# A one-layer decoder trunk on one core: compressed weights turned in a scores' bank, query splits in other slots, the first MLP chunk's groups in turn, the last factors taken in later, and products of zeros first

## The chip, the cores and the metric

The kernel runs on one core of a Trainium2 chip, as one program. The metric is device microseconds of one execution, as a median over runs. Engines are TensorE (PE; its weight loads are listed as PEld), VectorE (DVE), ScalarE (ACT), GpSimd (POOL) and SyncE (SP), which mostly issues DMAs. All times are in microseconds.

## What is computed

The input x is 512 tokens by 1024 channels, float32, one layer:

```python
h = rms_norm(x, norm_mix[l])
proj = h @ w_in[l]
u, q, kc, vc, ksl, vsl, kwn, vwn, g_nsa, g_merge = jnp.split(proj, IN_SPLITS, axis=-1)
y_pool = pool_mixer(u, w_pool[l], pool_scale[l])
y_nsa = nsa_mixer(q, kc, vc, ksl, vsl, kwn, vwn, g_nsa, ...)
merged = g_a * (y_pool @ w_proj_pool[l]) + g_b * (y_nsa @ w_proj_nsa[l])
x = x + merged @ w_out[l]
h = rms_norm(x, norm_mlp[l])
x = x + jnp.square(jax.nn.relu(h @ w_ff1[l])) @ w_ff2[l]
return rms_norm(x, norm_final)          # after the layer
```

The second mixer has 16 heads of 64 channels in 2 key groups and three branches: compressed keys and values (31 blocks of 32 tokens), selected blocks and a window, each with its softmax and gate. With 8 blocks of 64 tokens and up to 16 to be selected, every causal block is taken, so both other branches are causal attention over all 512 tokens, with keys of their own. The MLP has a hidden width of 4096.

## The kernel before

Every float32 operand of a product is split in two: a high part (fp32r) and a low part, the rest. A product is three matmuls: high by high, high by low, low by high. ACT writes the high part (`wh`, lines 304 and 350) and DVE the low part (`wl`, lines 306 and 352; POOL does some of these while `mode["pool"]` is set). A weight arrives by DMA in a tile `raw`, is split by `emit_prep_half` some steps before its use, and is taken by `use`.

The code is written as generators in a list `side`; `step_side` lets each of them make one step, up to its next `yield`. How many yields stand between two operations sets how far apart they are written. A scheduler then orders the instructions of each engine, and each engine runs its own in that order.

The stages, in order:

1. Start. x arrives, `ones` by `grow` (line 521) spreads the first norm's gain over 128 partitions in PSUM (`psM`), DVE scales x by it, PE turns x (line 548) and the first products follow (line 450).
2. Projections of `w_in`, 128 output channels at a time: 24 matmuls of 128x512 each (line 393). The last of them are left over as filler (`fill`) for the attention stage. A query is rotated (`rope`, with DMAs that swap quarters, `rs<-rx`) and split (`split_q`: ACT line 654, DVE line 656).
3. Attention, 8 pairs of heads with 12 slots each. Slot i: scores on PE in a bank of tag S (`score_pe`, line 1024; S has three banks), the mask and the smallest on DVE (`smax`, line 1049), the exponential on ACT (`expo`), the scale by gate and sum on POOL (`weight`, line 1075). LAG slots later PE turns the weights in a bank of tag T (`turn_pe`, line 1092; T has two banks), ACT and DVE split them (`PT`, lines 1103 and 1107), and PLAG later come the products with the values (`pv`, line 1126). Compressed branch: `cmp_scores` of the next pair starts at slot 4 of each pair; eight small matmuls (line 961), the softmax on DVE, ACT and POOL (lines 968 to 987, into `PC`, high and low part), then four transposes (line 993) and a copy by ACT (`pc`, one buffer), which `pv` takes with `VC` (line 1117) as the first product of a pair's halves. Filler matmuls are spread over the slots by count.
4. The projection of the attention's output, the merge, the output product and the second norm.
5. The MLP in 4 chunks of the hidden width, each with 2 groups. Both MLP products are done over 2 by 2 blocks with seven block products instead of eight, on sums of blocks; products are called A11, A12, S1, S2, S3, S4, A22. In the first product (`Group`, line 1395) sums of the input T1 to T4, in the second (`Wide`, line 1512) sums of the hidden blocks (`yT1` to `yT4`), are made by DVE and split again. For the first chunk the order of block products is in `FIRST`, for the others in `IN_TURN`:

```python
FIRST = ("A11", "A12"), ("S1", "S3", "S2"), ("A22", "S4")
IN_TURN = ("A11", "S3", "S1", "S2", "A12", "A22", "S4")
```

6. The end. `Wide.take` adds finished block products to x (lines 1529 and 1533), `fold` the sums (line 1540), `gained` (POOL, line 1574) multiplies a part of x by the last norm's gain, and per 128 tokens the square sums, the root, the last scale and the store follow.

Of the kernel before, what the change touches and what calls it, by code (L numbers as in the profile page):

```python
# [13 lines left out]
F32 = mybir.dt.float32  # L14
FR = mybir.dt.float32r
# [5 lines left out]
S = 512  # L21
DFF = 4096
NH = 16
NPAIR = NH // 2
# [38 lines left out]
def trunk(ctx: ExitStack, tc: tile.TileContext, A, out):  # L63
# [73 lines left out]
    LAST = 3  # L137
# [53 lines left out]
    for c in range(4):  # L191
        of = [add_group(1, c, g) for g in range(2)]
        if c == 0:
            turn = [(g, o) for os in FIRST[:1] for o in os for g in range(2)]
            turn += [(g, o) for os in FIRST[1:] for g in range(2) for o in os]
        else:
            turn = [(g, o) for g in range(2) for o in IN_TURN]
        add_turn(1, c, of, turn)
        of = [add_group(2, c, g) for g in range(2)]
        seen = {}  # L200
        turn = []
        for o in OUT_TURN if c < LAST else [o for o in LAST_TURN for g in range(2)]:
            g = seen.get(o, 0)
            seen[o] = g + 1
            turn.append((g, o))
        add_turn(2, c, of, turn)
# [310 lines left out]
    identR = cp.tile([128, 128], FR, name="identR")  # L517
    POOL.memset(ones, 1.0)
    psg = [ps1.tile([128, 512], F32, tag="M", bufs=2, name="psM") for _ in range(2)]
    for h in range(2):  # L520
        PE.matmul(psg[h], ones, grow[:, 512 * h:512 * h + 512], start=True, stop=True)

# [123 lines left out]

    Q_BUFS = 4

    def split_q(p, q):

        t = ap.tile([128, 2, S], FR, tag="Q", bufs=Q_BUFS, name="Q")
        for h in range(2):
            r, c = slice(64 * h, 64 * h + 64), slice(64 - 64 * h, 128 - 64 * h)
            ACT.activation(t[r, h, :], q[r, :], AF.Copy)
            yield
            DVE.tensor_tensor(t[c, h, :], q[r, :], t[r, h, :].bitcast(F32), op=ALU.subtract)
            yield
        Q[p] = t

    def turned_q(p):  # L660
# [5 lines left out]
        return None if p < Q_BUFS else oT[:, p, :]  # L666

    def later_q(p):
        yield from split_q(p, oT[:, p, :])

    with ExitStack() as c1:
        p1 = c1.enter_context(pool("p1"))
# [228 lines left out]
    with ExitStack() as c2:  # L901
        p2 = c2.enter_context(pool("p2"))
        ps2 = c2.enter_context(pool("ps2", space=PSUM))
        def fill2():
            for k in FILL2:
                i = int(k[-1])

                def post(ps, i=i, a=k[1] == "a"):
                    if not a:
                        ACT.activation(GB[:, i, :], ps, AF.Tanh, scale=0.5)  # L910
                        return
                    ACT.activation(ps, ps, AF.Tanh, scale=0.5)
                    DVE.scalar_tensor_tensor(MA[:, i, :], ps, 1.0, MA[:, i, :], op0=ALU.add, op1=ALU.mult)
                yield from fm(k, ps2, post)
            free.append(True)
            split_ready()
            early[0] = use("pn0") + (ps2.tile([128, S], F32, tag="F", bufs=F_BANKS, name="psF"),)
            for k in range(7):
                while (k, 1) not in split:
                    yield True  # L920
                proj_k(early[0], k)
                if k % 2 or k == 6:
                    ahead()
                    yield
# [31 lines left out]
        def cmp_scores(p):  # L956
            g = p // 4
            ps = ps2.tile([128, NT, 2, 64], F32, tag="S", bufs=S_BANKS, name="psC")
            for qb in range(NT):
                for h in range(2):  # L960
                    PE.matmul(ps[:, qb, h, :], Q[p][:, h, 128 * qb:128 * qb + 128], KC[g], start=True, stop=True,
                              skip_group_check=True)
            w = p2.tile([128, NT, 2, 64], F32, tag="cw", bufs=1, name="cw")
            s8 = p2.tile([128, 3, 8], F32, tag="c8", bufs=1, name="c8")
            cm = cst[:, C_CM:C_CM + 128].rearrange("p (q n) -> p q n", q=NT)
            wl = w[:, :, :, 0:32]
            wf = w.rearrange("p q h n -> p (q h) n")[:, :, 0:32]
            DVE.tensor_tensor(wl, ps[:, :, :, 0:32], cm[:, :, None, :].to_broadcast([128, NT, 2, 32]), op=ALU.add)
            sc = ps.rearrange("p q h n -> p (q h) n")[:, :, 0:32]
            DVE.tensor_tensor(ps[:, :, :, 0:32], ps[:, :, :, 32:64], wl, op=ALU.add)  # L970
            yield
            DVE.tensor_reduce(s8[:, 0, :], sc, axis=AX.X, op=ALU.min)
            DVE.tensor_tensor(wf, sc, s8[:, 0, :, None].to_broadcast([128, 8, 32]), op=ALU.subtract)
            yield
            yield
            yield
            ACT.activation(wl, wl, AF.Exp, scale=-1.0)
            yield
            DVE.tensor_reduce(s8[:, 1, :], wf, axis=AX.X, op=ALU.add)
            DVE.reciprocal(s8[:, 2, :], s8[:, 1, :])  # L980
            r = s8[:, 2, :].rearrange("p (q h) -> p q h", q=NT)
            DVE.tensor_tensor(r, r, GT[:, :, 6 * p:6 * p + 6:3], op=ALU.mult)
            yield
            POOL.tensor_tensor(wl, wl, r[:, :, :, None].to_broadcast([128, NT, 2, 32]), op=ALU.mult)
            pH, pL = (PC[:, :, e, :].rearrange("p q (h n) -> p q h n", h=2) for e in range(2))
            POOL.tensor_scalar(pH, wl, 1.0, 1.0, op0=ALU.mult, op1=ALU.mult)
            POOL.tensor_tensor(pL, wl, pH.bitcast(F32), op=ALU.subtract)
            for _ in range(6):
                yield
            pt = ps2.tile([128, S], F32, tag="T", bufs=T_BANKS, name="psT")  # L990
            for qb in range(NT):
                src = PC[:, qb, :, :].rearrange("p e c -> p (e c)")
                PE.transpose(pt[:, 128 * qb:128 * qb + 128].bitcast(FR), src, identR)
            t = p2.tile([128, S], FR, tag="pc", bufs=1, name="pc")
            ACT.activation(t, pt, AF.Copy)
            PTc[p] = t
# [152 lines left out]
        for i in range(n + LAG + PLAG):  # L1149
            if i < n:  # L1150
                p = slots[i][0]
                if i % 12 == 11 and Q_BUFS <= p + 2 < NPAIR:
                    side.append(later_q(p + 2))
                assert i % 12 != CMP_AT or p + 1 == NPAIR or p + 1 in Q
                if i % 12 == CMP_AT and p + 1 < NPAIR:
                    side.append(cmp_scores(p + 1))
# [330 lines left out]
    class Wide:  # L1487
# [33 lines left out]

        def take(self, o, ps):
            yield
            for f in range(2):
                if o in ("A11", "S2"):
                    if o == "A11" and self.c == 0:
# [18 lines left out]
    for c in range(4):  # L1545
        Y = Hidden()
        gs = [Group(c, g, Y) for g in range(2)]
        if c == 0:
# [3 lines left out]
            while not turned[0]:  # L1552
                step_side()
            for os in FIRST[1:]:
                for g in gs:
                    for o in os:
                        g.pe(o)
        else:
            for g in gs:
# [20 lines left out]
    def ending():  # L1580
# [4 lines left out]
        DVE.tensor_tensor(x, x, wide.ps["d"][1], op=ALU.add)  # L1585
        for t in (2, 3):
            square_sum(t, 1, 1)
            gained(t, 1)
            yield
        while "A12" not in wide.done:  # L1590
            yield
        for t in (0, 1):
            square_sum(t, 0)
            gained(t, 0)
            yield
        while "A22" not in wide.done:
            yield
        for t in (0, 1):
# [70 lines left out]
```

## Time and profile before

| | |
|---|---|
| median of 3 runs | 796.45 us (795.88 to 797.59) |
| the profiled execution | 794.17 us, with a span of 792.4 us |
| instructions | 12818 |
| PE, PEld, DVE, ACT, POOL busy | 98%, 85%, 78%, 62%, 23% of the span |
| DMA | 142.33 MB, mean 180 GB/s |

The profile is of one execution by the hardware profiler; its row starts count from the span's start. A row of the timeline has the start, the duration, engine, line, operation, output <- input, shapes and count, and in brackets the idle time of the engine just before it with what ended that. Rows of one group that follow each other are joined (x4). Matmuls are pipelined: the duration of one (0.40 for 128x512) is longer than the distance to the next (0.23), and ends are modelled. In what follows a row of a waits list has the total, the count and the longest wait. The costliest groups of PE, DVE, ACT and POOL, with busy time and mean ns of one, then the idle time before them:

```profile
L393 PE MATMUL psF<-R,wh 128*128 128x512 f32 x512 | 165.1, 402 | 0.0
L306 DVE TENSOR_TENSOR wl<-raw,wh 128x1024 fp32r<-128x1024 f32 x75 | 93.0, 1242 | 22.5 <-ACT wh L304 22.4
L304 ACT ACTIVATE wh<-raw 128x1024 fp32r<-128x1024 f32 x75 | 79.2, 1058 | 83.0 <-PE psB L1512 30.3
L1075 POOL TENSOR_SCALAR P<-P,sm,GT 128x128 f32<-128x128 f32 (+3 forms) x128 | 82.7, 674 | 52.7 <-DVE sm L1065 33.3
```

### The profile page before, as it was taken

Reading aid. Unit: us, or ns where it says so; the run is one execution under the profiler, and the core shown is the slowest. Engines: PE = TensorE matmul, PEld = TensorE weight load, DVE = VectorE, ACT = ScalarE, POOL = GpSimd, SP = SyncE. Lnnn points to the kernel's source line nnn. Section 1 sums busy time; section 2 is a strip of 40 time slices with the busy share of each in tenths; the row PEclk is TensorE's granted clock in tenths of the full one; section 3 lists DMA queues with packets and bytes.
Section 4 is the critical chain, followed back from the end, with each engine's and each line's share of the span. In section 5 each row is a group of like instructions: output and inputs, shape, how many; then the busy total and the mean of one; then the engine's idle time right before and its main releaser. Section 6 shows DMA issues by size and latency. Waiting matters only on the chain. (4 is left out here: it accounts for less than half of the span.)

```text
span 792.4 us, 12818 instructions
## 1 busy us (share of the span) xinstructions
PE 775.0 (98%) x4541; PEld 674.0 (85%) x4541; DVE 620.2 (78%) x1176; ACT 489.2 (62%) x962; POOL 181.2 (23%) x246
## 2 busy tenths in 40 slices
PE   8999999999999999999999999999999999999995
PEld 6889877888888888888888899978997899799974
DVE  6888666445999888887655579997889788978897
ACT  6756543335998888896334575944773477347744
POOL 4000000025876665664100100101110110100002
PEclk9999999999999999999999999999999999999998
DMA  9554743487753344334966607999999997987552
GB/s 306 136 153 120 197 110 100 127 213 185 134 108 81 81 95 120 80 81 115 300 155 198 163 1 199 331 238 289 281 262 233 288 282 217 276 240 241 175 171 107
DMA packets 116154, 142.33 MB, mean 180 GB/s; under 512 B 5525, under 2 KB 88121, under 8 KB 115898
## 3 DMA queue, kind: packets, MB, share of 16 engines
q1 hardware_dynamic: 97690, 117.72, 46.1%
q0 software_dynamic: 18112, 23.07, 19.3%
q10 hardware_dynamic: 288, 0.72, 0.3%
q8 instruction: 36, 0.59, 0.3%
q14 instruction: 28, 0.23, 0.1%
HBM read 136.77 MB, written 48.23 MB: 233 GB/s over the span
## 5 line engine op out<-in xcount | busy, mean ns | idle before, releaser
L393 PE MATMUL psF<-R,wh 128*128 128x512 f32 x512 | 165.1, 402 | 0.0
L304 ACT ACTIVATE wh<-raw 128x1024 fp32r<-128x1024 f32 x75 | 79.2, 1058 | 83.0 <-PE psB L1512 30.3
L271 POOL DMA_DIRECT2D S<-w_ff x44 | 48.7, 1107 | 356.5 <-DMA S<-w_ff 240.5
L350 ACT ACTIVATE wh<-raw 128x512 fp32r<-128x512 f32 (+1 forms) x100 | 60.1, 620 | 85.5 <-PE psF L393 45.4
L306 DVE TENSOR_TENSOR wl<-raw,wh 128x1024 fp32r<-128x1024 f32 x75 | 93.0, 1242 | 22.5 <-ACT wh L304 22.4
L393 PEld LDWEIGHTS psF<-R,wh 128*128 128x128 f32 x512 | 92.3, 188 | 17.9
L393 PE MATMUL psF<-R,wl 128*128 128x512 f32 x256 | 101.2, 395 | 0.0
L1075 POOL TENSOR_SCALAR P<-P,sm,GT 128x128 f32<-128x128 f32 (+3 forms) x128 | 82.7, 674 | 52.7 <-DVE sm L1065 33.3
L352 DVE TENSOR_TENSOR wl<-raw,wh 128x512 fp32r<-128x512 f32 (+1 forms) x84 | 56.9, 684 | 26.0 <-ACT wh L350 25.8
L1059 ACT ACTIVATE P<-P,sm 128x128 f32<-128x128 f32 (+3 forms) x128 | 71.0, 557 | 8.1 <-DVE sm L1049 7.5
L1049 DVE CUSTOM_DVE_ANT_0 P<-psS,cst 128x128 f32<-128x128 f32 (+3 forms) x128 | 59.5, 483 | 9.8 <-PE psT L1092 5.9
L1395 PE MATMUL psB<-R,wh 128*128 128x256 f32 x352 | 64.1, 282 | 0.0
L304 ACT ACTIVATE w3h<-raw 128x1024 fp32r<-128x1024 f32 x37 | 39.1, 1057 | 37.4 <-PE psB L1512 15.1
L1107 DVE TENSOR_TENSOR PT<-psT,PT 128x512 fp32r<-128x512 f32 (+2 forms) x96 | 56.9, 598 | 5.7 <-ACT PT L1103 4.8
L393 PEld LDWEIGHTS psF<-R,wl 128*128 128x128 f32 x256 | 48.1, 188 | 11.2
L1103 ACT ACTIVATE PT<-psT 128x512 fp32r<-128x512 f32 (+2 forms) x96 | 49.4, 520 | 11.5 <-PE psT L1092 10.2
L1395 PEld LDWEIGHTS psB<-R,wh 128*128 128x128 f32 x352 | 54.3, 189 | 0.5 <-DVE R L1337 0.2
L306 DVE TENSOR_TENSOR w3l<-raw,w3h 128x1024 fp32r<-128x1024 f32 x37 | 45.9, 1240 | 9.0 <-ACT w3h L304 8.9
L1092 PE MATMUL psT<-ident,P 128*128 128x128 f32 x320 | 50.7, 273 | 1.7 <-POOL P L1075 1.0
L1395 PE MATMUL psB<-R,wl 128*128 128x256 f32 x176 | 49.5, 281 | 0.0
L1092 PEld LDWEIGHTS psT<-ident,P 128*128 128x128 f32 x320 | 39.4, 140 | 10.4 <-issue 2.1
L1126 PE MATMUL psO<-PT,VV 128*128 128x256 f32 x320 | 47.7, 286 | 0.0
(381 smaller groups left out, 2005.7 us busy)
## 6 DMA issues: line engine op xcount, KB each, us to landing
raw<-w_ff SPq DMA_DIRECT2D x54, 512.0 KB, 5.9
S<-w_ff POOLq DMA_DIRECT2D x44, 512.0 KB, 7.8
raw<-S SPq DMA_DIRECT2D x44, 512.0 KB, 4.4
raw<-w_in SPq DMA_DIRECT2D x32, 512.0 KB, 4.0
S<-w_ff SPq DMA_DIRECT2D x32, 512.0 KB, 5.8
S<-S SPq DMA_DIRECT2D x12, 512.0 KB, 5.4
raw<-w_proj_nsa SPq DMA_DIRECT2D x8, 512.0 KB, 3.9
raw<-w_out SPq DMA_DIRECT2D x8, 512.0 KB, 4.9
```

Of the source, the lines that this page charges most:

```text
L304: ACT.activation(h, t, AF.Copy)
L306: DVE.tensor_tensor(l, t, h.bitcast(F32), op=ALU.subtract)
L350: ACT.activation(h[:, sl], t[:, sl], AF.Copy)
L352: eng.tensor_tensor(l[:, sl], t[:, sl], h[:, sl].bitcast(F32), op=ALU.subtract)
L393: PE.matmul(ps, a, b, start=first and j == 0, stop=last and j == n - 1, skip_group_check=True)
L1049: DVE.tensor_tensor_reduce(out=P[:, o:o + n].rearrange("p (a c) -> p a c", c=128), in0=s, in1=m, scale=1.0, scalar=3e38, op0=ALU.add, op1= ...
L1059: last_exp[:] = [ACT.activation(c, c, AF.Exp, bias=sm[:, 0, e:e + 1], scale=-1.0, accum_out=sm[:, 1, e:e + 1])]
L1075: r = POOL.tensor_scalar(P[:, o:o + n], P[:, o:o + n], sm[:, 2, e:e + 1], GT[:, qb, c + e:c + e + 1], op0=ALU.mult, op1=ALU.mult)
L1092: PE.transpose(pt[:, 128 * j:128 * j + 128], P[:, 128 * j:128 * j + 128], ident)
L1103: ACT.activation(dH, src, AF.Copy)
L1107: DVE.tensor_tensor(dL, src, dH.bitcast(F32), op=ALU.subtract)
L1395: PE.matmul(out, w[u][:, k, 128 * f:128 * f + 128], XB[x][v][:, k, :], **kw)
```

## The change

Six edits, in the order of the program:

- DVE sets a tile `zeros` (128x512) to zero, and PE multiplies it by itself six times into a bank of tag F ahead of the gain's matmuls. The result is not used.
- In the compressed branch the four transposes take a bank of tag S in place of T, and stand two yields behind the last operation on POOL instead of six.
- Queries of pairs 4 on are split from slot 7 instead of slot 11 of an earlier pair, with two yields more between the halves.
- `mode["pool"]` ends with the filler's last projection, so that DVE and not POOL makes the low parts of the weights that follow.
- In the MLP's first chunk the two groups alternate within each block product, instead of one group's three (or two) products and then the other's.
- At the end `take` of A12 in the last chunk waits five steps, and `gained` of the second halves of tokens 256 to 511 stands behind that of the first halves of tokens 0 to 255.

Line numbers behind the first edit grow by 10 to 17: in the changed kernel the transposes are line 1006, the turns 1105, the products with `VC` 1130, the scores 1037, `take` 1545 and 1549.

```diff
@@ -192,7 +192,7 @@
         of = [add_group(1, c, g) for g in range(2)]
         if c == 0:
             turn = [(g, o) for os in FIRST[:1] for o in os for g in range(2)]
-            turn += [(g, o) for os in FIRST[1:] for g in range(2) for o in os]
+            turn += [(g, o) for os in FIRST[1:] for o in os for g in range(2)]
         else:
             turn = [(g, o) for g in range(2) for o in IN_TURN]
         add_turn(1, c, of, turn)
@@ -517,6 +517,16 @@
     identR = cp.tile([128, 128], FR, name="identR")
     POOL.memset(ones, 1.0)
     psg = [ps1.tile([128, 512], F32, tag="M", bufs=2, name="psM") for _ in range(2)]
+    zeros = p0.tile([128, 512], FR, name="zeros")
+    DVE.memset(zeros.bitcast(F32), 0.0)
+    psw = ps1.tile([128, 512], F32, tag="F", bufs=2, name="psF")
+
+    def stir(n):
+
+        for _ in range(n):
+            PE.matmul(psw, zeros[:, 0:128], zeros, start=True, stop=True)
+
+    stir(6)
     for h in range(2):
         PE.matmul(psg[h], ones, grow[:, 512 * h:512 * h + 512], start=True, stop=True)
 
@@ -646,7 +656,7 @@
 
     Q_BUFS = 4
 
-    def split_q(p, q):
+    def split_q(p, q, gap=0):
 
         t = ap.tile([128, 2, S], FR, tag="Q", bufs=Q_BUFS, name="Q")
         for h in range(2):
@@ -655,6 +665,8 @@
             yield
             DVE.tensor_tensor(t[c, h, :], q[r, :], t[r, h, :].bitcast(F32), op=ALU.subtract)
             yield
+            for _ in range(gap if h == 0 else 0):
+                yield
         Q[p] = t
 
     def turned_q(p):
@@ -666,7 +678,7 @@
         return None if p < Q_BUFS else oT[:, p, :]
 
     def later_q(p):
-        yield from split_q(p, oT[:, p, :])
+        yield from split_q(p, oT[:, p, :], 2)
 
     with ExitStack() as c1:
         p1 = c1.enter_context(pool("p1"))
@@ -913,6 +925,7 @@
                     DVE.scalar_tensor_tensor(MA[:, i, :], ps, 1.0, MA[:, i, :], op0=ALU.add, op1=ALU.mult)
                 yield from fm(k, ps2, post)
             free.append(True)
+            mode["pool"] = False
             split_ready()
             early[0] = use("pn0") + (ps2.tile([128, S], F32, tag="F", bufs=F_BANKS, name="psF"),)
             for k in range(7):
@@ -985,9 +998,9 @@
             pH, pL = (PC[:, :, e, :].rearrange("p q (h n) -> p q h n", h=2) for e in range(2))
             POOL.tensor_scalar(pH, wl, 1.0, 1.0, op0=ALU.mult, op1=ALU.mult)
             POOL.tensor_tensor(pL, wl, pH.bitcast(F32), op=ALU.subtract)
-            for _ in range(6):
-                yield
-            pt = ps2.tile([128, S], F32, tag="T", bufs=T_BANKS, name="psT")
+            yield
+            yield
+            pt = ps2.tile([128, S], F32, tag="S", bufs=S_BANKS, name="psT")
             for qb in range(NT):
                 src = PC[:, qb, :, :].rearrange("p e c -> p (e c)")
                 PE.transpose(pt[:, 128 * qb:128 * qb + 128].bitcast(FR), src, identR)
@@ -1149,7 +1162,7 @@
         for i in range(n + LAG + PLAG):
             if i < n:
                 p = slots[i][0]
-                if i % 12 == 11 and Q_BUFS <= p + 2 < NPAIR:
+                if i % 12 == 7 and Q_BUFS <= p + 2 < NPAIR:
                     side.append(later_q(p + 2))
                 assert i % 12 != CMP_AT or p + 1 == NPAIR or p + 1 in Q
                 if i % 12 == CMP_AT and p + 1 < NPAIR:
@@ -1521,6 +1534,9 @@
 
         def take(self, o, ps):
             yield
+            if o == "A12" and self.c == LAST:
+                for _ in range(5):
+                    yield
             for f in range(2):
                 if o in ("A11", "S2"):
                     if o == "A11" and self.c == 0:
@@ -1552,8 +1568,8 @@
             while not turned[0]:
                 step_side()
             for os in FIRST[1:]:
-                for g in gs:
-                    for o in os:
+                for o in os:
+                    for g in gs:
                         g.pe(o)
         else:
             for g in gs:
@@ -1585,7 +1601,6 @@
         DVE.tensor_tensor(x, x, wide.ps["d"][1], op=ALU.add)
         for t in (2, 3):
             square_sum(t, 1, 1)
-            gained(t, 1)
             yield
         while "A12" not in wide.done:
             yield
@@ -1593,6 +1608,8 @@
             square_sum(t, 0)
             gained(t, 0)
             yield
+        for t in (2, 3):
+            gained(t, 1)
         while "A22" not in wide.done:
             yield
         for t in (0, 1):
```

## The prediction

> **What bounds the kernel now.** I read the busy shares first, then what TensorE (PE) waits for in each stage, then the rows around each wait. Starts and durations are in us.
>
> ```profile
> span 792.4 us, 12818 instructions
> PE 775.0 (98%) x4541; PEld 674.0 (85%) x4541; DVE 620.2 (78%) x1176; ACT 489.2 (62%) x962; POOL 181.2 (23%) x246
> ...
> 200.00:375.00 175.00, 171.16 (x1131) 151.54 (x1130) 154.82 (x485) 150.49 (x408) 114.04 (x161) 1.00 0.45 97
> 784.30:792.40 8.10, 0.01 (x1) 0.00 (x0) 3.18 (x9) 3.10 (x9) 0.00 (x0) 0.66 0.61 240
> ```
>
> PE is busy for 98% of the span: an edit can win only PE's pauses, some cold work at the start, and the 8.1 us behind its last matmul. The two lower lines are stretches (length; busy PE, weight loads, DVE, ACT, POOL; granted clock; DMA share): the attention stage, where DVE and ACT are also at 88% and 86%, and the end. The waits of PE, from three stretches (200 to 375, 470 to 525, 740 to the end; total, times, longest):
>
> ```profile
> PE psT L993 <- DVE PT L1107: 1.9, 6, 0.5
> PE psT L1092 <- POOL P L1075: 1.0, 1, 1.0
> PE psT L1092 <- DVE PT L1107: 0.7, 3, 0.3
> ...
> PE psB L1395 <- ACT wh L304: 0.6, 1, 0.6
> PE psB L1512 <- DVE yT3L L1450: 0.5, 1, 0.5
> ...
> PE psB L393 <- DVE wl L306: 0.7, 1, 0.7
> ```
>
> Ends of matmuls are modelled, so these understate: I size a pause from starts, as the distance between two groups less what the same group takes elsewhere.
>
> **Part 1, compressed weights' transposes (CT), pair 0.** With two yields for six, CT comes earlier in PE's order. Before the first score there are 72 filler matmuls (L393) between the compressed scores (L961) and CT; now 49. On PE, start of the attention stage, before:
>
> ```order
> L393 MATMUL psF<-R_63,wl_1703 128x512
> L993 MATMUL psT<-identR,PC 128x128 x4
> L393 MATMUL psF<-R_63,wh_1743 128x512
> L393 MATMUL psF<-R_64,wh_1743 128x512
> L393 MATMUL psF<-R_63,wl_1744 128x512
> ```
>
> And now:
>
> ```order
> L393 MATMUL psF<-R_63,wh_1711 128x512
> L1006 MATMUL psT<-identR,PC 128x128 x4
> L393 MATMUL psF<-R_64,wh_1711 128x512
> L393 MATMUL psF<-R_63,wl_1712 128x512
> L393 MATMUL psF<-R_63,wh_1711 128x512
> ```
>
> CT moved ahead by 23 fillers, which now run inside the attention stage; its input PC has not moved on the other engines:
>
> ```profile
> 168.39 0.97 PE L961 MATMUL psC<-KC,Q 128*128 128x64 f32 x8
> 169.20 0.70 PE L393 MATMUL psF<-R,wh 128*128 128x512 f32 x2
> ...
> 186.07 0.46 PE L993 MATMUL psT<-identR,PC 128*128 128x128 f32 x4
> ...
> 175.88 0.69 DVE L619 TENSOR_TENSOR rx<-rx,cst 128x512 f32<-128x512 f32 x1 [6.12 <-DMA rs<-rx]
> 179.40 0.41 DVE L968 TENSOR_TENSOR cw<-psC,cst 128x256 f32<-128x256 f32 x1
> ...
> 184.22 0.74 POOL L987 TENSOR_TENSOR PC<-cw,PC 128x256 fp32r<-128x256 f32 x1
> ```
>
> A filler costs (186.07 - 169.20) / 72 = 0.234, so PE reaches CT at 169.20 + 49 x 0.234 = 180.7. PC is complete at 184.96, behind a chain that starts with a DMA (rs, landed 175.9) and passes DVE in order: the compressed softmax (L968) stands behind the rotation of the last query. PE waits 4.3, with nothing else in its order: **+4.3**. The 23 fillers are moved, not saved. Ends: DVE stood idle 6.12 for that DMA; a landing 2 sooner makes it +2.3, one a little later +5.
>
> What a pause costs beyond its length is in the end row above: clock 0.66 over 8.1 us without a matmul is (1 - 0.66) / 0.5 x 8.1 = 5.5 us at half, so the grant fell some 2.6 after PE stopped. A pause of 4.3 is long enough by that row; pauses up to 1 left it at 1.00 between 200 and 375. Coming back took, at the start (rows below), from the first transposes at 6.95 to about 11.8 at half rate: 4.8, of which half, 2.4, is lost. So 0 to +2.4, and as the pause falls differently in each run I take the middle, **+1.2**. [...]
>
> **Part 2, the same transposes inside the stage.** They left the T banks (two) for the S banks (three), and from among the compressed scores of the next pair to behind the turns of slot 1. PE, pair 3, before:
>
> ```order
> L1024 MATMUL psS<-KH_124,Q 128x384
> L1024 MATMUL psS<-KL_126,Q 128x384
> L1092 MATMUL psT<-ident,P 128x128 x4
> L961 MATMUL psC<-KC_131,Q 128x64 x6
> L993 MATMUL psT<-identR,PC 128x128 x4
> L961 MATMUL psC<-KC_131,Q 128x64 x2
> ```
>
> And now:
>
> ```order
> L1037 MATMUL psS<-KH_124,Q 128x256
> L1037 MATMUL psS<-KL_126,Q 128x256
> L1105 MATMUL psT<-ident,P 128x128 x4
> L1006 MATMUL psT<-identR,PC 128x128 x4
> L1130 MATMUL psO<-pc,VC_132 128x2x128
> L1130 MATMUL psO<-pc,VC_133 128x2x128
> L1139 MATMUL psO<-PT,VV 128x256 x6
> ```
>
> CT now stands right ahead of the products with VC of the pair before; the wait for a T bank is gone.
>
> ```profile
> 212.33 0.64 PE L961 MATMUL psC<-KC,Q 128*128 128x64 f32 x5
> 213.06 0.54 PE L993 MATMUL psT<-identR,PC 128*128 128x128 f32 x4
> ...
> 251.68 0.49 PE L1117 MATMUL psO<-pc,VC 128*128 128x256 f32 x2
> ...
> 282.27 0.72 PE L961 MATMUL psC<-KC,Q 128*128 128x64 f32 x5
> 283.49 0.51 PE L993 MATMUL psT<-identR,PC 128*128 128x128 f32 x4 [0.50 <-DVE PT L1107]
> ...
> 246.62 0.74 POOL L987 TENSOR_TENSOR PC<-cw,PC 128x256 fp32r<-128x256 f32 x1
> 207.34 0.74 POOL L987 TENSOR_TENSOR PC<-cw,PC 128x256 fp32r<-128x256 f32 x1
> 207.19 0.40 PE L1117 MATMUL psO<-pc,VC 128*128 128x256 f32 x2
> ```
>
> An L961 needs about 0.1 (eight in 0.81 at 168.39), so CT at 283.49 waited 1.22 - 0.5 = 0.7 where the row has 0.50 of idle time, and CT at 213.06 waited 0.2 where it has none: each idle time is 0.2 short. With it the waits of L993 are 1.9 + 6 x 0.2 + 0.2 = 3.3. In pair 3 PC is there (247.36) 4 us ahead of the new place (251.68); in pair 1 it is not: PC ends at 208.08, the place is at 207.19. That gives back 0.9. Banks S can stall the score behind, since CT holds one until ACT has copied it: up to 0.5 in a pair, the longest T wait; I take 0.5 in all.
>
> By the same reckoning the T waits of L1092 are 0.7 + 3 x 0.2 = 1.3, and its wait for POOL 1.0 + 0.2 = 1.2. That one is at 370:
>
> ```profile
> 367.56 1.77 POOL L352 TENSOR_TENSOR wl<-raw,wh 128x512 fp32r<-128x512 f32 x1 [2.90 <-ACT wh L350]
> ```
>
> There POOL's split of a weight, 1.77 long, stands ahead of the softmax weights that PE waits for. With mode["pool"] off at the fill's end the split moves to DVE, which PE does not wait for there. The moved Q splits change which DVE work lies ahead of the L1092 waits; and the 23 fillers (5.4 of PE) lie in the later pairs, so DVE and ACT gain slack against PE. Pauses before: 3.3 + 1.3 + 1.2 = 5.8; back come 0.9 + 0.5: **-4.4**. Ends: -5.8 and, if DVE sets the pace and the pauses only move, 0.
>
> **Part 3, first MLP chunk.** Groups alternate within a product, so T3 and T2 (DVE sums of inputs, then splits) have one product more, 24 matmuls of 0.117, or 2.8, before they are wanted.
>
> ```profile
> 475.89 0.70 PE L1395 MATMUL psB<-R,wh 128*128 128x256 f32 x2
> 476.43 0.28 PE L1395 MATMUL psB<-xT3H,w3h 128*128 128x256 f32 x1
> 477.84 0.39 PE L1395 MATMUL psB<-xT2H,wh 128*128 128x256 f32 x1 [0.65 <-ACT wh L304]
> ...
> 480.00:525.00 45.00, 44.53 (x300) 40.47 (x299) 42.61 (x54) 30.93 (x44) 5.80 (x5) 1.00 1.00 273
> ```
>
> From 475.89 to 477.84 four matmuls (one at xT3L is not shown) take 1.95 for 0.47: 1.5 lost, all of it covered now. But the last products of group 0 come later, so the output sums start later on a DVE that is busy 42.6 of the 45 us from 480 to 525; its wait for yT3L (0.5 above) may grow by up to 2. I take **-1.2**, ends -2.0 and +0.5.
>
> **Part 4, the end.** DVE, from the second last pair of weights on, before:
>
> ```order
> L306 TENSOR_TENSOR w3l<-raw_4860,w3h 128x1024
> L1272 TENSOR_SCALAR sq<-sq 128x1
> L1533 TENSOR_TENSOR x_4485<-x_4485,psB 128x512 x2
> L306 TENSOR_TENSOR wl_4909<-raw_4838,wh_4908 128x1024
> L1272 TENSOR_SCALAR sq<-sq 128x1 x2
> ```
>
> And now:
>
> ```order
> L306 TENSOR_TENSOR w3l<-raw_4895,w3h 128x1024
> L1285 TENSOR_SCALAR sq<-sq 128x1
> L1549 TENSOR_TENSOR x_4494<-x_4494,psB 128x512
> L306 TENSOR_TENSOR wl_4918<-raw_4847,wh_4917 128x1024
> L1549 TENSOR_TENSOR x_4494<-x_4494,psB 128x512
> ```
>
> The last split (wl) moved ahead of one addition, and POOL's products with the last gain, which slow DVE, behind most of the splits.
>
> ```profile
> L306 DVE TENSOR_TENSOR wl<-raw,wh x75: 1215/1223/2059, 434.7 to 778.0; 128x1024 fp32r<-128x1024 f32 x75
> 777.60 3.52 POOL L1574 TENSOR_TENSOR MA<-x,GB 128x512 f32<-128x512 f32 x2 [1.82 <-DVE x L1533]
> 778.04 1.93 DVE L306 TENSOR_TENSOR wl<-raw,wh 128x1024 fp32r<-128x1024 f32 x1
> 780.03 0.50 PE L393 MATMUL psB<-wl,y22H 128*128 128x512 f32 x1 [0.74 <-DVE wl L306]
> ```
>
> Beside POOL a split takes 1.9 for 1.22. Free of that the last one ends over 1.3 sooner, and PE's pause at 780.03 (0.9 by starts) goes. POOL's products, now later, can slow the last additions. **-0.8**, ends -1.3 and 0.
>
> **Part 5, six products of zeros.**
>
> ```profile
> 3.21 3.75 PE L521 MATMUL psM<-grow,ones 1*128 1x512 f32 x4 [3.21 <-DMA grow<-norm_mix]
> 6.95 3.67 PE L548 MATMUL psTr<-ident,x 128*128 128x128 f32 x16
> 9.04 2.50 POOL L352 TENSOR_TENSOR wl<-raw,wh 128x512 fp32r<-128x512 f32 x2
> 10.55 1.85 PE L450 MATMUL psF<-R,wh 128*128 128x256 f32 x8
> 12.23 1.10 PE L450 MATMUL psF<-R,wl 128*128 128x256 f32 x8
> 13.18 1.11 PE L450 MATMUL psF<-R,wh 128*128 128x256 f32 x8
> ...
> 0.82 0.10 DVE L800 MEMSET oT<- 128x16 f32 x2 [0.82 <-PEq L1660]
> ```
>
> Eight 128x256 take 1.68 from 10.55, 0.95 from 12.23: the first twelve microseconds run at half rate, and there a 128x512, twice the columns, costs 0.42 to 0.46. DVE's memset of 128x512 takes between 0.10 (L800) and 0.69 (L619, as wide) from 0.9 on; then come six products, to about 4.1, 0.9 behind the landing of grow. If PE then is fast some 4 us sooner, the transposes save 1.7 and the first eight products 0.8; POOL's low factors (to 11.54) cap the gain near 1.2. If not, it costs 0.9. I take **-0.7**, near the cap less a little, since PE then has products of all 128 rows in place of a wait.
>
> **Sum.** +4.3 + 1.2 - 4.4 - 1.2 - 0.8 - 0.7 = -1.6 on the profiled execution of 794.17 (792.4 of span). That one lies 2.3 below the median, outside the three runs; the difference is set against the median: 796.45 - 1.6 = 794.85. A difference under 0.2%, 1.6, is about what cannot be told from none.
>
> **Rivals.** A (chance 0.28): the pause comes but leaves the clock alone, as the pauses of 1 did: without the 1.2, -2.8, 793.65. B (0.10): the pause is covered, since DMA rs lands soon after its issue and DVE's chain starts 4 sooner; without 4.3 and 1.2, -7.1, 789.35. Against it: DVE's and POOL's order behind that DMA is as it was, and the queues are no emptier. C (0.20), slower: DVE paces the attention stage, so that its 4.4 do not come and the pause of part 1 stays: -1.6 + 4.4 = +2.8, 799.25. It decides from the point where less than 1.2 of the 4.4 is left. DVE's 88% in a stage where PE has 98% speaks against it; the late PC of pair 1, which hangs on DVE, for it. The forecast has 0.42, from -2.8 to +0.5.
>
> Faster by over 0.2%: B, nearly all of A (0.26) and 0.16 of the forecast, 0.52; slower: 0.15 of C and 0.02 of the forecast, 0.17; within: 0.31. The range goes from B's edge (half of B left out) into C (under half of it left out): 790.0 to 798.8.
>
> **What would show it.** In the profile after: PE idle of about 4 ahead of the first L1006, released by POOL L1000; a granted clock under 1 just behind it, or doubled matmul spacing; no waits of L1006 for DVE; a pause of about 1 at the second L1006; no pause at xT3 and xT2; the last splits at 1.22; transposes of x at 0.11. I am wrong if PC is ready at 181, or if the T waits come back at L1105.

## The result, and the profile after

| | before | changed |
|---|---|---|
| median | 796.16 us (794.46 to 797.59, 6 runs) | 804.66 us (803.61 to 806.68, 6 runs) |
| ratio | 1 | 1.0114, 95% interval 1.0094 to 1.0133 |
| profiled execution, span | 794.17, 792.4 | 806.19, 804.3 |

The change made the kernel 9.1 us slower by the ratio (1.14% of 796; the medians differ by 8.5); -1.6 had been predicted. The two profiled executions differ by 12.0, since that of before lies 2.0 under its median and the other 1.5 over.

The page of the changed kernel, first lines:

```profile
span 804.3 us, 12841 instructions
PE 781.0 (97%) x4547; PEld 679.3 (84%) x4547; DVE 622.0 (77%) x1178; ACT 490.1 (61%) x962; POOL 178.8 (22%) x245
```

Apart from PE's six products of zeros no engine has more work to speak of: the time is pauses of PE and work at half rate. The waits of PE in the changed kernel, from 180 to 390 and from 470 to 530 (total, times, longest), against the five rows of the same stages before:

```profile
PE psT L1006 <- POOL PC L1000: 7.2, 3, 4.6
PE psS L1037 <- DVE cw L986: 1.2, 1, 1.2
PE psT L1105 <- DVE PT L1120: 0.4, 1, 0.4
...
PE psB L1408 <- DVE MA L1429: 1.8, 1, 1.8
PE psB L1408 <- DVE MA L1432: 1.3, 1, 1.3
PE psB L1408 <- ACT wh L304: 1.0, 1, 1.0
PE psB L1525 <- ACT yT1H L1460: 0.6, 1, 0.6
```

In the attention stage the waits for DVE's PT are gone, as meant, but waits for PC have come: 4.6 in pair 0, and 2.6 in two more; before the stage had 3.6 in all, now, without the 4.6, 4.2. In the first MLP chunk 1.1 became 4.7. Around pair 0 of the changed kernel, on DVE, POOL and PE, and then the stretch behind it (length; busy PE, weight loads, DVE, ACT, POOL; granted clock; DMA share; GB/s):

```profile
177.62 0.69 DVE L629 TENSOR_TENSOR rx<-rx,cst 128x512 f32<-128x512 f32 x1 [6.43 <-DMA rs<-rx]
186.09 0.72 POOL L1000 TENSOR_TENSOR PC<-cw,PC 128x256 fp32r<-128x256 f32 x1
181.89 0.40 PE L393 MATMUL psF<-R,wh 128*128 128x512 f32 x1
186.87 0.75 PE L1006 MATMUL psT<-identR,PC 128*128 128x128 f32 x4 [4.58 <-POOL PC L1000]
...
186.80:191.50 4.70, 4.63 (x16) 3.96 (x17) 0.94 (x8) 1.94 (x7) 1.29 (x2) 0.51 0.07 8
```

This is the pause that part 1 worked out: the last filler begins at 181.89, PC is complete at 186.81. Behind it PE is busy for 4.6 us at a granted clock of 0.51, so up to 2.3 are lost (from 191.5 on the clock is 1.00 again); against e11 below, where the same products run at full rate, it is 1.8.

At the start, the changed kernel's PE rows, to be held against the L521, L548 and L450 rows of the prediction's part 5:

```profile
1.46 2.93 PE L527 MATMUL psF<-zeros 128*128 128x512 f32 x6 [1.46 <-DVE oT L812]
4.32 3.78 PE L531 MATMUL psM<-grow,ones 1*128 1x512 f32 x4
8.03 3.74 PE L558 MATMUL psTr<-ident,x 128*128 128x128 f32 x16
```

The gain's products begin 1.1 later, and sixteen transposes still take 3.74 (3.67 before), 0.23 each: no full rate there, against 0.12 for each of the eight of the same line at 13.80 in e12 (0.95 to the next row).

### The profile page after: what moved, and what is told of

The parts are those of the page before. It is cut to its first block, busy times and chain, and to the rows that moved or that the text cites. A ratio compares the mean times of both kernels' runs of the same rounds, so it can differ in the third digit from the quotient of the medians.

```text
span 804.3 us, 12841 instructions
## 1 busy us (share of the span) xinstructions
PE 781.0 (97%) x4547; PEld 679.3 (84%) x4547; DVE 622.0 (77%) x1178; ACT 490.1 (61%) x962; POOL 178.8 (22%) x245
## 5 line engine op out<-in xcount | busy, mean ns | idle before, releaser
L304 ACT ACTIVATE wh<-raw 128x1024 fp32r<-128x1024 f32 x75 | 79.2, 1058 | 78.7 <-PE psB L1525 31.4
L306 DVE TENSOR_TENSOR wl<-raw,wh 128x1024 fp32r<-128x1024 f32 x75 | 92.3, 1233 | 21.7 <-ACT wh L304 21.6
L352 DVE TENSOR_TENSOR wl<-raw,wh 128x512 fp32r<-128x512 f32 (+1 forms) x85 | 60.4, 716 | 23.3 <-ACT wh L350 23.1
L304 ACT ACTIVATE w3h<-raw 128x1024 fp32r<-128x1024 f32 x37 | 39.1, 1057 | 42.7 <-PE psB L1408 14.9
L306 DVE TENSOR_TENSOR w3l<-raw,w3h 128x1024 fp32r<-128x1024 f32 x37 | 45.9, 1240 | 12.9 <-ACT w3h L304 12.9
L1105 PE MATMUL psT<-ident,P 128*128 128x128 f32 x320 | 50.3, 273 | 0.4 <-DVE PT L1120 0.4
L1105 PEld LDWEIGHTS psT<-ident,P 128*128 128x128 f32 x320 | 39.5, 140 | 8.3 <-POOL P L1088 0.7
```

The costliest lines, as they stand in the source:

```text
L304: ACT.activation(h, t, AF.Copy)
L306: DVE.tensor_tensor(l, t, h.bitcast(F32), op=ALU.subtract)
L352: eng.tensor_tensor(l[:, sl], t[:, sl], h[:, sl].bitcast(F32), op=ALU.subtract)
L1105: PE.transpose(pt[:, 128 * j:128 * j + 128], P[:, 128 * j:128 * j + 128], ident)
```

## The experiments

Thirteen kernels, each the kernel before with a part of the change or a variant of it. "Before" is the run of the kernel before on the same chip.

| run | what it has | median, before | ratio (95%) |
|---|---|---|---|
| e1_zeros | products of zeros | 795.66, 796.06 | 0.9999 (0.9984 to 1.0014) |
| e2_ct | S bank and two yields | 802.74, 796.06 | 1.0088 (1.0069 to 1.0108) |
| e3_alt | first chunk's groups alternate | 800.10, 796.06 | 1.0052 (1.0037 to 1.0068) |
| e4_tail | the end's edits | 794.72, 796.06 | 0.9985 (0.9975 to 0.9995) |
| e7_q_pool | query splits, mode pool off | 793.97, 795.14 | 0.9985 (0.9976 to 0.9995) |
| e5_ct_hold | e2, pair 0 with six yields | 793.05, 795.37 | 0.9971 (0.9961 to 0.9981) |
| e8_sbank6 | S bank alone | 793.42, 795.37 | 0.9980 (0.9965 to 0.9994) |
| e11_filled | e2, the pause filled | 799.71, 795.14 | 1.0057 (1.0040 to 1.0074) |
| e6a_alt_three | S1, S3, S2 alternate | 794.77, 795.37 | 0.9991 (0.9979 to 1.0003) |
| e6b_alt_two | A22, S4 alternate | 796.72, 795.37 | 1.0015 (1.0005 to 1.0025) |
| e9_s4_first | all alternate, S4 ahead of A22 | 795.68, 795.14 | 1.0009 (0.9999 to 1.0018) |
| e12_best | bank, yields, e7, end | 791.43, 794.79 | 0.9955 (0.9942 to 0.9969) |
| e13_best_zeros | e12 and the zeros | 792.40, 794.79 | 0.9970 (0.9960 to 0.9980) |

**The five parts alone.** Each has one group of the change's hunks, shortened here:

```diff
+    for _ in range(6): PE.matmul(psw, zeros[:, 0:128], zeros, start=True, stop=True)      # e1
-            pt = ps2.tile([128, S], F32, tag="T", bufs=T_BANKS, name="psT")               # e2, and two yields for six
+            pt = ps2.tile([128, S], F32, tag="S", bufs=S_BANKS, name="psT")
-            turn += [(g, o) for os in FIRST[1:] for g in range(2) for o in os]            # e3, and the loop like it
+            turn += [(g, o) for os in FIRST[1:] for o in os for g in range(2)]
+            if o == "A12" and self.c == LAST:                                             # e4, and gained later
+            mode["pool"] = False                                                          # e7, and the two hunks on later_q
```

e1_zeros: 

> The kernel before with only the six products of zeros. Theory: in the profile after, they held the gain's matmuls back by 1.1 us and the full rate did not come sooner, so this part alone costs 1.0 to 1.5 us (797.2 to 797.7) and the transposes of x still take 0.21 us each. Rival (the prediction's part 5): products of zeros bring the full rate some us earlier in most executions and the profile after showed an unlucky one; then 0.7 us faster (795.5).

e2_ct: 

> The kernel before with only the compressed weights' transposes moved: a bank of tag S, two yields. Theory: PE waits for PC in pairs 0, 1 and 2 (4.7, 1.3 and 1.7 us in the profile after), once for a bank of tag S (1.3), and the granted clock falls to half for some 7 us behind the first; against that the waits for DVE's PT (3.3) go: 4 to 7 us slower (800 to 803). Rival: the waits of pairs 1 and 2 come from the other edits (query splits in other slots, POOL's split moved), and this one alone costs only the pause of pair 0 and the clock less the waits saved: 1 to 3 us slower (797 to 799).

e3_alt: 

> The kernel before with only the two groups alternating in the first MLP chunk. Theory: the sums of weights come later, so buffers of raw come free later and the loads behind them land later; PE waits 1.4 and 1.9 us there as in the profile after, with the clock at half for one stretch of 3.4 us: 3 to 5.5 us slower (799 to 801.5). Rival 1: the late loads came from DMA traffic that the earlier edits had shifted by 8 us, and the order alone saves 1.2 us as predicted (795). Rival 2: DVE's sums of the output are late (part 3's lower end): PE waits at yT3, under 2 us in all, and the loads are on time.

e4_tail: 

> The kernel before with only the end's edits (take of A12 waits, gained later). Theory: as predicted and as the profile after shows from the last chunk on, 0.8 to 1.0 us faster (795.2 to 795.4), the last splits at 1.22 us. Rival: the end after was faster only because its DMAs were spread otherwise; then no change and POOL's work slows the last additions.

e7_q_pool: 

> The kernel before with only the query splits' new slots and mode pool off at the fill's end. Theory: PE's wait for POOL near 370 (1.1 us) goes, since the split of a weight moves from POOL to DVE; the waits for PT at the turns (1.3) are those that the query splits move: 1.1 to 2.4 us faster (793.7 to 795). Rival: the waits only change place, since DVE has the split now: within 0.5 of before.

In units of 796: 0 + 7.0 + 4.1 - 1.2 - 1.2 = +8.7, against 9.1 for the whole. Two parts make the loss, and they make it alone: the same waits stand in the profiles of e2 (pair 0 4.3, pairs 1 and 2 1.3 and 1.7 by starts, the S bank 1.3) and, with 0.6 for the 1.3, of e3 (1.8, 1.0, 0.6, 0.6). So rival and rival 1 there, which laid them on the other edits, are out, and so is e3's rival 2: no wait for yT3 is left in it. e4 and e7 are as expected; in e7 PE's wait for POOL is gone, while the three waits for PT at the turns are as before (0.7 in all), so the query splits' slots did nothing that shows. e1 was at odds with its profile, which has the gain's products 1.1 late as after; it is taken up again in e13.

**The transposes' place and their bank.** e8 changes one word, e5 has the yields depend on the pair, e11 fills the pause:

```diff
-            pt = ps2.tile([128, S], F32, tag="T", bufs=T_BANKS, name="psT")
+            pt = ps2.tile([128, S], F32, tag="S", bufs=S_BANKS, name="psT")     # e8, e5, e11
-            for _ in range(6):
+            for _ in range(6 if p == 0 else 2):                                 # e5; e11: 2
                 yield
...
+            for _ in range(0 if p else 18):                                     # e11
+                PE.matmul(pt, identR, hT[0][:, 0, :], start=True, stop=True)
```

e8_sbank6: 

> The kernel before with only the bank's tag changed (S for T), six yields as before. Theory: the wait is for a bank, not for the data; with three S banks PE's seven waits for DVE's PT ahead of the transposes (3.3 us by starts) go, and at most 1 comes back at the scores: 2 to 3 us faster (793 to 794). Rival: the S banks are as full, the scores behind the transposes wait as long (1.3 us once in the profile after): within 0.7 us of before.

e5_ct_hold: 

> The transposes' move alone, as in the run before last of its kind, but pair 0 keeps six yields, so 72 fillers stand ahead of its transposes again. Theory: the pause of 4.3 us and the fall of the clock (1.7 us) go, the waits for PC in pairs 1 and 2 (1.3 and 1.7) and for the S bank (1.3) stay, and the waits for PT that it removes (3.3) stay removed: 795 to 797 against 796.1 before. Rival: the waits of pairs 1 and 2 follow from the pause (with PE's 23 fillers moved), and go with it: 791 to 793.

e11_filled: 

> The transposes' move alone (two yields, a bank of tag S, as in the second run), with 18 more products of 128x512 right ahead of pair 0's transposes, in the bank that the transposes then overwrite; their result is not used. They fill 4.2 of the 4.3 us for which PE waits for PC and change nothing else. Theory: the pause's length is DVE's and POOL's, so PC comes at the same time, but the clock does not fall behind it: 1.5 to 2.2 us faster than that run, 800 to 801, and no stretch at half rate behind 186. Rival: the fall of the granted clock has no price, since PE waits in the following slots anyway: within 0.7 us of that run.

PE's waits from 180 to 380 in e8, then the longer ones in e5, then in e11:

```profile
PE psT L1092 <- POOL P L1075: 1.0, 1, 1.0
PE psT L1092 <- DVE PT L1107: 0.7, 3, 0.3
PE psO L1117 <- ACT P L1059: 0.5, 1, 0.5
PE psC L961 <- DVE sm L1049: 0.2, 1, 0.2
...
PE psT L993 <- POOL PC L987: 1.1, 1, 1.1
PE psO L1117 <- DVE oT L1135: 0.8, 2, 0.5
...
PE psT L995 <- POOL PC L987: 3.5, 3, 1.3
PE psS L1026 <- DVE cw L973: 1.2, 1, 1.2
```

e8: the bank alone takes all waits of L993 away (1.9 in the waits before) and gives 0.7 back; its time, -1.6 by the ratio, is a little under the 2 to 3 expected. The rival is out by the waits; the time's interval, -2.8 to -0.5, just reaches it. e5: -2.3, better than the theory and short of the rival. The pause and the fall of the clock are gone, as both said (no wait of PE over 1.1 in the stage; mean granted clock 0.996 in its profile, 0.994 in e2's); of the three other waits only pair 1's stays, so those of pair 2 and of the S bank came from pair 0's new place.

e11: in its profile the granted clock stays at 1.00 from 182 to 196, and the other waits of e2 are left; PC came 1.0 later than in e2's profile, so that 1.0 of the pause remained. Behind the pause PE has the same products in both, from pair 0's transposes to the next compressed scores (e2, then e11):

```profile
184.89 0.53 PE L993 MATMUL psT<-identR,PC 128*128 128x128 f32 x4 [4.18 <-POOL PC L987]
195.69 0.97 PE L961 MATMUL psC<-KC,Q 128*128 128x64 f32 x8
...
185.92 0.54 PE L995 MATMUL psT<-identR,PC 128*128 128x128 f32 x4 [1.01 <-POOL PC L987]
195.40 0.97 PE L961 MATMUL psC<-KC,Q 128*128 128x64 f32 x8
```

They take 10.80 in e2 and 9.48 in e11, so the fall of the clock costs 1.3 there; in the changed kernel they take 11.25 (186.87 to 198.12), 1.8 more. Counted from the transposes e2 is still 1.5 behind e11 at the stage's last product, so the following slots do not absorb it, and the rival is out. By the times e11 is 2.5 us faster than e2 (0.31% of 796, ratio against ratio), with the two intervals together 0.4 to 4.5, which alone would not exclude the rival's 0.7.

e11 also shows that the waits of pair 2 and of the S bank do not hang on the idle time, which is mostly filled there, but on the place of the 23 fillers. In pair 2 of the changed kernel DVE has

```profile
221.79 2.06 DVE L352 TENSOR_TENSOR wl<-raw,wh 128x512 fp32r<-128x512 f32 x1
223.78 0.41 DVE L986 TENSOR_TENSOR cw<-psC,c 128x256 f32<-128x256 f32 x1
```

The split of a filler's weight, 2.06 long while POOL splits too (from 222.02), stands ahead of L986, which frees the S bank and leads to PC. In e2 and e11 it takes 2.03 and 2.05, in e5 0.67, and before no split stands there.

On PE the attention stage, from pair 0's compressed scores to the start of the last product with values, takes 207.4 before; by the profiles it is 5.8 longer in e2, 5.1 longer in e11, and shorter by 2.0 in e5, 1.8 in e8, 1.0 in e7 and 2.5 in e12.

**The first MLP chunk.** Which of the two alternations costs the time, and what it is that PE waits for:

```diff
-            turn += [(g, o) for os in FIRST[1:] for g in range(2) for o in os]
+            # e6a: o outermost for ("S1", "S3", "S2") only; e6b: for ("A22", "S4") only
-    FIRST = ("A11", "A12"), ("S1", "S3", "S2"), ("A22", "S4")
+    FIRST = ("A11", "A12"), ("S1", "S3", "S2"), ("S4", "A22")     # e9, o outermost throughout
```

e6a_alt_three: 

> The kernel before with the groups alternating in S1, S3, S2 of the first chunk only; A22 and S4 group by group as before. Theory: DVE's sum that gives a raw buffer back (line 316) stands two splits later, the load behind it lands later, DVE stands behind the split of that load, and PE waits for the sums behind it: the late load is there as in the alternation of all five (ACT waits about 5 us for raw), and it costs 1 to 4 us (797 to 800). Rival: it is the second alternation (A22 of group 1 right behind A22 of group 0) that makes PE wait; then this one is 0.5 to 1.2 us faster than before.

e6b_alt_two: 

> The kernel before with the groups alternating in A22 and S4 of the first chunk only. Theory: the raw buffers come free as before, DVE is not held up, and the shorter notice for A22 of group 1 costs under 0.7 us: 795.5 to 796.8. Rival: the notice is what counts: PE waits about 2 us for DVE's sums at A22 of group 1 and the time is 2 to 4 us longer (798 to 800).

e9_s4_first: 

> The first chunk's groups alternate in all five products, but S4 of both groups stands ahead of A22 of both. S4's weights are made from sums and need no load, so A22 of group 1 is wanted two products (5.6 us) later than in the alternation of the change. Theory: what made PE wait 3 us there is the load of A22's weights, which can only begin when a raw buffer is given back, and DVE standing behind its split: with S4 ahead the wait goes and the time is 0.5 to 2 us under before (794 to 795.5). Rival: it is the notice for DVE's sums u2 and u3, whatever the loads do; S4 needs them still earlier than A22, and PE waits 2 to 4 us at S4 (798 to 800).

In e9 S4's sum overwrites a term before A22's sum reads it, so a part of the hidden layer has other values; instructions and sizes are those of e3. My theory had the wrong alternation: e6a costs nothing (its interval holds no change), e6b costs 1.2 by the ratio, less than the rival's 2 to 4. Its profile is of the slowest of its ten executions, 2.2 above their median, so the wait in it is longer than usual: PE stands 2.9 for DVE, with the granted clock at 0.53 behind it. DVE and ACT there (lines stand three further down in this kernel; L309 and L307 are the splits), PE's wait, the stretch behind it, and, last, two rows of before: the split that stood at this place in DVE's order, and ACT's row for the load of A22 of group 1:

```profile
497.12 1.06 ACT L307 ACTIVATE w3h<-raw 128x1024 fp32r<-128x1024 f32 x1 [3.73 <-DMA raw<-w_ff]
498.21 1.23 DVE L309 TENSOR_TENSOR w3l<-raw,w3h 128x1024 fp32r<-128x1024 f32 x1 [4.08 <-ACT w3h L307]
500.07 0.69 DVE L1419 TENSOR_TENSOR MA<-psB,MA 128x512 f32<-128x512 f32 x1
...
PE psB L1398 <- DVE MA L1419: 2.9, 1, 2.9
501.00:504.30 3.30, 3.30 (x17) 3.30 (x18) 3.22 (x4) 1.77 (x4) 0.00 (x0) 0.53 1.10 242
...
493.79 1.23 DVE L306 TENSOR_TENSOR w3l<-raw,w3h 128x1024 fp32r<-128x1024 f32 x1 [0.24 <-ACT w3h L304]
495.16 1.06 ACT L304 ACTIVATE wh<-raw 128x1024 fp32r<-128x1024 f32 x1 [1.40 <-DMA raw<-w_ff]
```

In e6b w3 are the weights of A22 of group 1. They come by DMA, the load lands near 497, ACT waits for it 3.7 and DVE 4.1, and behind DVE's split stands the sum u3 (L1419) that empties the bank of PE's next product. Before, the split ahead of that sum was that of S4 of group 0, whose weights are made from sums and not loaded (w3 there, at 493.79). The load of A22 of group 1 landed near 495.2, and PE wanted it at 500.3; in e6b PE wants it at 497.9, a product sooner. Why it also lands later was not taken apart. e9 puts both S4 ahead of both A22: the waits of 1.8 and 1.3 in the changed kernel shrink to

```profile
PE psB L1512 <- DVE w3l L306: 1.2, 1, 1.2
PE psB L1395 <- ACT wh L304: 1.0, 1, 1.0
PE psB L1395 <- DVE MA L1419: 0.5, 1, 0.5
```

and the rival (still longer waits at S4) is out. But it is not under before either: 1.2 come back in the second product, at w3l. That the load and the split in DVE's order cause the wait is shown by e6b's rows and by e9; that the alternation of S1, S3, S2 adds to it when both are there (e3 costs 4.1, e6a and e6b together 0.5) is only seen, its cause was not taken apart. In e3's profile the waits are 2.9 more than before (4.0 for 1.1), and A22 of group 1 behind them takes 4.5 for 2.8, with the granted clock at 0.53 over 3.3 of it: 4.5 together.

**Together, and the zeros once more.**

```diff
-            for _ in range(6):
+            for _ in range(6 if p < 2 else 2):         # with the S bank, e7's and the end's edits
                 yield
```

e12_best: 

> All edits of the change that gained alone: the S bank, two yields from pair 2 on (six in pairs 0 and 1, so that PE does not reach the transposes ahead of PC), the query splits' slots, mode pool off, and the end's edits; the first MLP chunk and the start as before. Theory: the parts add up, since each takes a wait of PE of its own: -2.3 to -3 for the bank and yields, -1.2 for POOL's split, -1.2 for the end: 4.5 to 6 us faster than before (789 to 791). Rival: with PE's other waits gone DVE and ACT pace the attention stage, and the waits come back at other places: 2 to 4 us faster (791 to 793).

e13_best_zeros: 

> The kernel above with the six products of zeros at the start. Theory: they take 2.9 us at half rate, less than a stretch of 3.4 us between changes of the granted clock, so they never bring the full rate by themselves; the gain's matmuls start 1.1 later and all behind them: 0.8 to 1.4 us slower than the kernel above. Rival: the timed runs of the zeros alone, within 0.15% of before on both sides, mean what they say: the start is hidden, and the two kernels agree within 0.4 us.

e12 is the fastest: 3.6 us under before. It is the rival's size (2.5 to 4.6): the parts' -2.3, -1.2 and -1.2 come to -4.7, but each has some 0.8 either way, so the shortfall is not clear of noise, and it was not taken apart. Its waits from 180 to 380 are few and short, the longer two:

```profile
PE psO L1120 <- DVE oT L1138: 0.7, 2, 0.5
PE psT L996 <- POOL PC L990: 0.5, 1, 0.5
```

e13 is 1.0 slower than e12 by the medians, 0.15% by the ratios, and its profile has PE 1.2 later at the start, 1.1 at the end of the attention stage and 0.5 at the end of the span. PE's first rows in e12 and in e13:

```profile
3.17 3.75 PE L521 MATMUL psM<-grow,ones 1*128 1x512 f32 x4 [3.17 <-DMA grow<-norm_mix]
6.85 3.73 PE L548 MATMUL psTr<-ident,x 128*128 128x128 f32 x16
...
1.47 2.93 PE L524 MATMUL psF<-zeros 128*128 128x512 f32 x6 [1.47 <-DVE oT L807]
4.32 3.77 PE L526 MATMUL psM<-grow,ones 1*128 1x512 f32 x4
8.03 3.74 PE L553 MATMUL psTr<-ident,x 128*128 128x128 f32 x16
```

The zeros do not bring the full rate for the transposes in any of the three profiles that have them (changed kernel, e1, e13: 3.74 for sixteen in each); they hold back the gain's products by 1.1. With e13 that fits the theory; e1's times (-0.1, interval -1.3 to +1.1) allow it, but do not show it. The theory's 3.4 is the length of a stretch at half rate in the changed kernel (508.9 to 512.3); that 2.9 is too short is its estimate from that length, and the 3.74 agree with it.

## Why the prediction was wrong

Term by term, against the single runs:

| term | predicted | measured |
|---|---|---|
| pause ahead of pair 0's transposes | +4.3 | 4.6 idle in the profile |
| the clock behind it | +1.2 (0 to 2.4) | 1.8 in the profile, 1.3 in e2's; 2.5 (0.4 to 4.5) by e11's times |
| pauses inside the stage | -4.4 for these and the split on POOL | +0.3 in e2's profile (stage 5.8 longer, less 4.2 and 1.3); e7 -1.2 |
| first MLP chunk | -1.2 | +4.1 (e3) |
| the end | -0.8 | -1.2 (e4) |
| zeros | -0.7 | +1.0 (e13); -0.1, from -1.3 to +1.1 (e1) |

Parts 2 and 3 make 3.5 and 5.3 of the 10.7 between forecast and result. Neither sign that the prediction named for being wrong showed (PC ready at 181, T waits back at L1105). Of its signs for being right two failed: a pause of 1.0 at xT3 is there, and the transposes of x take 0.23.

- **Part 1 was right** in place and length, read from one order and one chain: 72 fillers to 49, DMA, DVE, POOL. The price of the clock, +1.2, was half of the upper end, taken because the pause falls differently in each run, an estimate of mine that no run shows; by the rows it was 1.3 to 1.8, so the term was a little small but inside its range. In the three profiles with a pause of 2.9 to 4.6 in the attention stage or the first MLP chunk the grant fell to half: for 6.8 in the changed kernel (4.6), about 3.4 in e2 (4.2) and at least 3.1 in e6b (2.9). Rival A, which had the clock hold, is out.
- **Part 2 failed at its second step**, that PC is ready at the new place in the other pairs and that the moved fillers only give slack. I checked PC against the new place in pair 3 and in pair 1, gave back 0.9 for pair 1 and took the others as covered. The trace of before already had pair 2 late too (POOL's L987 and PE's place, L1117):

```profile
228.64 0.73 POOL L987 TENSOR_TENSOR PC<-cw,PC 128x256 fp32r<-128x256 f32 x1
...
228.63 0.48 PE L1117 MATMUL psO<-pc,VC 128*128 128x256 f32 x2
```

PC ends at 229.4, 0.7 behind the place. Measured were 1.3 and 1.7 by starts, and 1.3 for an S bank that the compressed scores held until DVE's L986; 0.9 + 0.5 were in the sum. e5 and e11 show that pair 2's and the S bank's share came with the 23 moved fillers, which I had counted only as slack gained: a split of a filler's weight, 2.06 for e5's 0.67, stood ahead of L986 on DVE. The bank itself did what was meant (e8), and rival C, that DVE paces the stage, is out: with pair 0's transposes in their old place e5 is 2.3 faster than before, and the stage 2.0 shorter.
- **Part 3 failed in its cover.** It counted the notice that T3 and T2 gain, and on the other side only DVE's output sums. The same row of the new order shortens the notice for A22 of group 1 from two products to one, and puts the split of its weights, which are loaded, ahead of group 1's sums on DVE; the prediction names no load there. And the gain was not there: the row at xT2H that I quoted named ACT's split of a weight (wh, L304) as what PE waited for, and I put the pause down to T2 and T3. Their earlier notice is of no use while ACT makes wh when it did: PE still waits 1.0 for it in the changed kernel, now at xT3H.
- **Part 4 was right**: no wait for L306 is left at the end, and the last split takes 1.22 in e4 and 1.21 in the changed kernel (rows) for 1.93. The reason given was half right: POOL's products still run beside two earlier splits, of 2.06 and 1.88, and beside the last too. But the last stands one addition sooner and begins 0.15 ahead of POOL's; before it began 0.44 behind them (778.04 against 777.60).

```profile
790.40 1.21 DVE L306 TENSOR_TENSOR wl<-raw,wh 128x1024 fp32r<-128x1024 f32 x1
790.55 3.47 POOL L1590 TENSOR_TENSOR MA<-x,GB 128x512 f32<-128x512 f32 x2 [1.82 <-DVE x L1549]
```

- **Part 5 failed in sign**, by e13: I took a value near the cap, because products of all 128 rows replaced a wait; they last 2.9, the products of one row behind them 3.7, and the transposes behind those still run at half rate. The range's other end, +0.9, is what e13 measured.

The range, 790.0 to 798.8, left out the case in which two parts fail together; the upper ends of its own terms, +5 + 2.4 + 0 + 0.5 + 0 + 0.9 = +8.8, would have held nearly all of it.

## What to carry to other kernels

When an order puts a consumer earlier, compare its new place with the end of its producer for every turn of the loop, the first above all, where nothing yet runs ahead; and count what the filler that it overtakes brings to the turns behind on the other engines, its weights' splits above all. When products change places, list for each of them the notice that it loses, its weights' load included, beside the notice that another gains: a late load costs the whole engine that stands in order behind its split (in e6b ACT waited 3.7 for it, DVE 4.1 and PE 2.9). In these profiles the pauses of PE of 4.2 and 4.6 us cost 1.3 and 1.8 more in clock.

## What the runs showed of the hardware

The granted clock fell to half behind pauses of PE of 4.6 (changed kernel, 0.51 over 4.7 us), 4.2 (e2, 0.61 over the 4.0 from 185) and 2.9 (e6b, 0.53 over 3.3 us). In e3 it fell behind two pauses of 0.7 and 1.8 with two matmuls between them (rows: the stretch with both, with PE busy 2.48 of 4.80, and the one behind, at 0.53), and in the changed kernel behind two of 1.3 and 1.8 at the same place. In the changed kernel it is 0.50 from 184.6 to 191.4, 6.8 long, where it begins inside the pause, 2.3 behind the end of the last filler (182.3), and from 508.9 to 512.3, 3.4 long. In e2 about 3.4 at half is an estimate from 0.61 over 185 to 189 and 0.97 over 189 to 193, (0.39 x 4 + 0.03 x 4) / 0.5; by the 0.71 over 185 to 187 it begins 1.0 behind the pause's end. In e6b 0.53 over 3.3 is 3.1 at half, by the same reckoning. Single pauses of 1.0 (e11) and of 1.1 and 1.5 (pairs 1 and 2 of the changed kernel) left the clock at 1.00. Six 128x512 products of zeros at the start, 2.9 us, did not bring the full rate to the transposes, 3.7 us later: sixteen take 3.74, and 3.67 before. That is read from the distances alone, since the profile puts the granted clock at 1.00 over the first 12 us, before and in the changed kernel.

```profile
496.00:500.80 4.80, 2.48 (x19) 2.10 (x18) 4.13 (x6) 3.80 (x5) 1.16 (x1) 1.00 0.75 253
500.90:504.20 3.30, 3.30 (x16) 3.30 (x17) 2.26 (x3) 2.74 (x6) 0.00 (x0) 0.53 1.17 226
```
